# A static order whose estimate puts ScalarE's table loads ahead of the instruction that needs them, with other ranks for the work woven into the projections

## The chip, the cores and the metric

The kernel runs on one core of a Trainium2 chip. The metric is the device time of one execution in microseconds (us). Engines are named as in the profile: PE (TensorE matmul), PEld (TensorE weight load), DVE (VectorE), ACT (ScalarE), POOL (GpSimd) and SP (SyncE, which issues the transfers).

## The reference

One inference step of a decoder trunk with two layers, on a prompt of 1024 tokens and eight samples of four tokens, model width 1024, all in float32.

```python
for layer in range(DEPTH):                       # 2: attention, then gated DeltaNet
    hp, gp = modulate(xp, c_prompt, ...)         # rms_norm(x) * (1 + scale(c)) + shift(c), and gate(c)
    hs, gs = modulate(xs, c_sample, ...)
    if layer % N_MIXERS == 0:
        op, kp, vp = swa_branch(hp, ...)         # q, k, v, z = h @ w_in (16 heads of 64, 4 kv heads)
        osm, ksm, vsm = swa_branch(hs, ..., cache_swa_k, cache_swa_v)
        #   softmax over the last 128 positions with a sink per head; (attn * silu(z)) @ w_out
    else:
        op, cp, sp = gdn_branch(hp, conv0, s0, ...)   # xqkv, z, a, b = h @ w_in; xqkv is 4096 wide
        osm, csm, ssm = gdn_branch(hs, state_gdn_conv, state_gdn_s, ...)
        #   silu(causal conv of 4 taps) gives q, k (8 heads of 128) and v (16 heads of 128);
        #   l2-normed q and k; the delta rule in chunks of 64 with a triangular solve each;
        #   (rms_norm(o) * silu(z)) @ w_out
    xp, xs = xp + gp * op, xs + gs * osm
y_prompt, y_sample = rms_norm(xp, final_norm_g), rms_norm(xs, final_norm_g)
```

The new keys and values, the conv tails and the DeltaNet states are outputs too.

## The kernel before

All 1056 tokens stand on the free axis in three column groups of 384, 384 and 288 (`GRP`). A projection takes 128 output columns at a time: for each group, 24 matmuls add into one bank of PSUM (tile ps_pj). They are 24 because each of the eight blocks of the inner axis is multiplied three times in a split of float32 into a high and a low part: wh with hhi, wh with hlo, wl with hhi (h2hi and h2lo in the second layer). The weights come by transfers into wr and are split into wh and wl by ScalarE and VectorE. A group that is done is evacuated by a function of its own (`evac`), and PE goes on in the next of the two ps_pj banks.

Everything else is woven into this stream of projection matmuls: attention of the heads done so far, the modulation vectors (cT times w_mod, four matmuls a step), the output projection of the attention layer, and in the second layer, for each of eight groups of heads hq, the conv taps, the decays, the chunks' triangular systems (tiles UZ, M, Xd, X), the chain of states (S, uo, ks, DP) and the outputs. Each such piece is a generator, which yields a condition and then issues the next few instructions. `weave` puts it into a list by its rank, and `stages` goes through the list from low ranks to high and runs whatever has its condition fulfilled; the projection calls it (`fetch`, `until`) between its matmuls. Ranks are the numbers in K, in KR for pieces of one head group, and in KT in place of K while the kernel closes.

The conditions come from an estimate that runs along as the program is written. Each instruction that is issued passes `Core.issued`, which is line 84's `call` in the profile for nearly every row. It keeps for every engine the time at which it is free (`self.free`), and for every tile when it was written and last used. `ready(tile)` holds when the estimate has the tile written by the time PE is free; `soon` and `idle` hold a little earlier or later and look at another engine. If the estimate says that a tile is late, PE's matmul on it is written behind more projection matmuls. The order is fixed once the program is built: at run time each engine takes its instructions in that order and waits on semaphores where the estimate was wrong.

ScalarE needs a table load when an Exp follows a Silu or the other way round (`TABLES`).

The pieces that come up below:

- In the second layer a v column goes from ps_pj to XR (a copy on ScalarE), through four taps into vT, then Silu in place (`taps`), and then `turn` transposes it on PE into ps_tr, with the identity in erl, and copies it to vo. There are three vT buffers (VB) and one ps_tr bank; `turn` gives both back.
- In the attention layer the key projection is read twice from its bank: ScalarE casts it to khh, VectorE takes the difference kll.
- Layer 1 is the DeltaNet layer. Its shift and scale come from `modulation_steps`, which multiplies cT by wm, four matmuls a step and eight steps, during the attention; `MM` paces it (a start and a distance, in projection matmuls). Its gate comes from `modulation_gate`, cT times wmod in four steps of four matmuls, during the attention's output projection; `MS` paces it. Behind each step the loads of the next are issued (`load(m + 1)`).
- `SW` is such a pace for the samples' states near the end, and `ORD` the order of q, k, v and z columns in each head group's round.

Of the kernel before, what the change touches and what calls it, by code (L numbers as in the profile page):

```python
# [93 lines left out]
class Core:  # L94
# [15 lines left out]
    def issued(self, eng, op, ins, args, kwargs):  # L110
# [10 lines left out]
        start = self.free[eng]  # L121
        for a in srcs:
            start = max(start, self.after(self.written, a, eng))
            if a.space == PSUM:
                start = max(start, self.after(self.used, a, eng))
        for a in outs:
            if self.used.get(self.key(a), (0.0, ""))[1] != "sync" or eng != "sync":
                start = max(start, self.after(self.used, a, eng))
        if "dma" in op:
            size = 4 * n * outs[0].shape[0] / 1e6  # L130
            rows = max(1, min(2 * outs[0].shape[0], n * outs[0].shape[0] // 16))
            self.free[eng] = start + 0.45
            self.moved = max(start + 0.7, self.moved) + 2.4 * size + 0.0005 * rows
            end = self.moved + self.dl[0 if outs[0].space == DRAM else 1]
        else:
            src = srcs[0] if srcs else outs[0]
            near = src.space == PSUM or srcs[-1].space == PSUM if srcs else False
            rate, fixed, over, seen = 960, 0.155, -0.083, 0.04
            if eng == "tensor":
                m, over, seen, fixed = outs[0].shape[0], 0.0, 0.18, 0.0  # L140
                new, self.group = self.group != outs[0].offset // outs[0].ap[0][0], outs[0].offset // outs[0].ap[0][0]
                if self.kind == "R":
                    rate, fixed = 2326, 0.008 + self.after_f
                    self.after_f = 0.0
                    self.wide_n = 0
                elif self.kind == "T":
                    rate = 1174
                elif m == P:
                    rate, fixed = 592, max(0.0, 0.22 - n / 592)
                elif m == 64:  # L150
                    rate, fixed = (1150 if new else 592), max(0.0, 0.068 - n / 1094)
                elif n >= 256:
                    rate, fixed = (1e9, 0.014) if new and self.wide_n == n else (1200, 0.126)
                elif new:
                    rate, fixed = 1e9, 0.014 if n == self.wide_n else 0.031 if self.wide_n < n else 0.076
                else:
                    rate, fixed = 560, 0.0
                if self.kind != "R":
                    wide = n >= 256 and m >= 64
                    self.after_f = 0.172 if wide else 0.086  # L160
                    self.tail = (-0.181 if wide else -0.08) if m == P else 0.04 if m == 64 else 0.12
                    self.wide_n = n if m < 64 else 0
            elif eng == "scalar":
                rate, fixed, over = 1200, 0.165 if near else 0.195, -0.1
                if any(getattr(kwargs.get(k), "space", None) is not None for k in ("scale", "bias")):
                    fixed += 0.09
                if kwargs.get("accum_out") is not None:
                    over += 0.18
                table = TABLES.get(args[2] if len(args) > 2 else None)
                if table and table != self.table:  # L170
                    self.table, over = table, over + 1.28
            elif eng == "gpsimd":
                rate, fixed, over = 420, 0.07 if n >= 256 else 0.14, 0.0
            elif op == "scalar_tensor_tensor":
                fixed = 0.207 if n > 16 else 0.15
            elif op.startswith("tensor_scalar") and src.space != PSUM:
                rate, fixed = 1920, 0.215 if any(hasattr(x, "tensor") for x in args[2:]) else 0.16
            elif op.startswith("tensor_scalar"):
                fixed = 0.207
            if op == "memset":  # L180
                rate = 1e9
            plain = "tensor_" in op and op not in ("tensor_copy", "tensor_reduce") and all(a.space != PSUM for a in aps)
            if op == "tensor_reduce":
                n *= srcs[0].shape[-1]
            if eng == "gpsimd" and plain:
                start = max(start, self.lock[2])
            elif eng == "vector" and plain and self.lock[0] <= start < self.lock[1]:
                start = self.lock[1]
            end = start + fixed + n / rate
            if eng == "gpsimd" and plain:  # L190
                self.lock[0:2] = start, end
            elif eng == "vector" and plain:
                self.lock[2] = end
            self.free[eng] = end + over
            end += seen
            if eng in self.last:
                self.tc.add_manual_dep(ins, self.last[eng],
                                       mybir.DependencyInfo(mybir.DependencyClass.NoSync, mybir.DependencyReason.DATA),
                                       reason="program order")
            self.last[eng] = ins.name  # L200
# [97 lines left out]
def body(tc, I, O, cst_ap, dbg=None):  # L298
# [21 lines left out]
    AT = (-5, 3)  # L320
    EX = (1.2, 1.6, 0, 0.9)
    ES, EN, EL, EM = EX
    K = {'split': 12, 'add': 26, 'attend': 22, 'turning': 24, 'modulate': 20, 'cached': 8, 'wo': 48, 'turn': 0, 'ahead': 2, 'taps': 2, 'gating': 6, 'decay': 23, 'samples': 28, 'load': 6, 'mod': 6, 'shape': 28, 'decays': 24, 'prepare': 60, 'gather': 23, 'finish': 24, 'states': 40, 'core': 10, 'new': 7}
    KT = {'prepare': 3, 'gather': 25, 'finish': 36, 'states': 10, 'core': 7, 'new': 9, 'load': 18, 'gating': 5, 'samples': 34, 'output': 11}
    KR = [{'chain': 4, 'output': 15, 'solve': 11, 'invert': 19, 'blocks': 31, 'decayed': 22}, {'chain': 31, 'output': 31, 'solve': 13, 'invert': 31, 'blocks': 39, 'decayed': 38}, {'chain': 32, 'output': 2, 'solve': 30, 'invert': 41, 'blocks': 2, 'decayed': 6}, {'chain': 35, 'output': 38, 'solve': 4, 'invert': 4, 'blocks': 0, 'decayed': 23}, {'chain': 9, 'output': 2, 'solve': 23, 'invert': 44, 'blocks': 1, 'decayed': 58}, {'chain': 41, 'output': 36, 'solve': 8, 'invert': 4, 'blocks': 58, 'decayed': 12}, {'chain': 8, 'output': 15, 'solve': 8, 'invert': 12, 'blocks': 58, 'decayed': 12}, {'chain': 10, 'output': 18, 'solve': 42, 'invert': 28, 'blocks': 1, 'decayed': 56}]
    TB = (3, 5)
    SW = (19, 7)
    MS = (54, 12)
    AH, AI = (a / 10 for a in AM)
    GP = (0, 0, 0, 0, 1)  # L330
    ORD = ['zzkv', 'zqzvk', 'zqzkv', 'qzzvk', 'qzzkv', 'vqzzk', 'qzzkv', 'qvzz']
    MM = (11, 4)
    ORDER = [("q", 2), ("q", 3), ("q", 4), ("q", 5), ("z", 0), ("k", 1), ("z", 1), ("z", 2), ("q", 6), ("q", 7),
             ("z", 3), ("z", 4), ("z", 5), ("z", 6), ("z", 7)]
    SE = ("vector", "vector", "vector", "vector")
# [99 lines left out]
    def modulation_gate(l, gw, nw, tag):  # L435
# [29 lines left out]
        def steps():  # L465
            load(0)
            for m in range(KD // 2):
                yield lambda: pos[0] >= MS[0] + MS[1] * (2 * m + 1)
                yield ready(*wts[m])
# [71 lines left out]
    def weave(gen, name, hq=None):  # L541

        rank = KT[name] if nc.closing and name in KT else KR[hq][name] if hq is not None else K[name]
        i = 0
# [466 lines left out]
    if True:  # L1011
# [305 lines left out]
        def cached_rows(b2):  # L1317
# [3 lines left out]
            vc = sa.tile([P, 2, 256], F32, tag="vc", name="vc", bufs=4)  # L1321
            KT = sa.tile([64, 2, 4, P], F32, tag="KT", name="KT", bufs=4)
            nc.sync.dma_start(KT.rearrange("p r h s -> p (r h s)"), I["keysT"][b2])
            nc.sync.dma_start(vc, vc_rows[bs].rearrange("b s c -> s b c"))
            return KT, vc

        def cached_pair(b2, smk, osv, held):

            yield lambda: paired[0] >= b2 - 2
            KT, vc = held[b2] if b2 < 2 else cached_rows(b2)  # L1330
            yield lambda: paired[0] >= b2 - 1
            yield ready(KT)
            lg = yield from bank("lg")
# [125 lines left out]
        load, step, end = modulation_gate(0, at, 8, "wg")  # L1459
# [10 lines left out]
        for t in range(NB + 1):  # L1470
# [3 lines left out]
            for k in range(KD):  # L1474
                hi, lo = wv[k // 2]
                for x, y in ((hhi, hi), (hlo, hi), (hhi, lo)):
                    with pinned():
                        mm = nc.tensor.matmul(pv, x[:, k, t * P:t * P + parts], y[:, k % 2, :],
                                              start=(n == 0), stop=(n == 23))
# [391 lines left out]
    plan = [0]  # L1871
    for r, order in enumerate(ORD):
        pz = [4096 + 2 * r * P, 4096 + (2 * r + 1) * P]
        blocks = {"q": [r * P], "k": [(HQ + r + 1) * P], "v": [2 * HQ * P + 2 * r * P, 2 * HQ * P + (2 * r + 1) * P]}
# [6 lines left out]
    if True:  # L1881
# [498 lines left out]
        states = {0: {}}  # L2380
# [270 lines left out]
        def states_times():  # L2651
# [34 lines left out]
            for u in range(0, len(us_), 2):  # L2686
                b, hd, _ = us_[u]
                if u % 16 == 0:
# [4 lines left out]
                    pk = yield from bank("mi")  # L2693
                yield lambda: pos[0] >= SW[0] + SW[1] * (u + 1) / 10
                yield sure(ES, sts[u], sts[u + 1], zq)
# [368 lines left out]
```

## Time and profile before

| | |
|---|---|
| three runs | 1606.88, 1610.4, 1607.8 us (median 1607.8) |
| profiled execution | 1610.62 us, 2.8 above the median |
| its span, first to last instruction | 1608.8 us; 1.8 us lie outside it |
| mean granted PE clock | 0.996 |
| PE busy | 1581.1 us, 98% |
| DVE, ACT, POOL busy | 76%, 52%, 9% |

A row of the timeline gives the start, the duration, the engine, the instruction with its output and inputs, and in brackets how long the engine had been idle and what ended that. The rows of waits give the engine, its tile, what it waited for, then the sum in us, the number of times and the longest. A busy share alone says little here: PE is the engine that everything is arranged around, so its idle time is what an order can change. fp32 matmuls that are one instruction in the program may show as two in the trace.

### The profile page before, as it was taken

The numbers are of one execution on the slowest core, as the hardware profiler recorded it, in microseconds if no ns is written. First come the engines' busy times: TensorE is split into PE (matmuls) and PEld (weight loads), VectorE is DVE, ScalarE is ACT, GpSimd is POOL, SyncE is SP. The second block draws the span as 40 slices with busy tenths as digits, with TensorE's granted clock in tenths as the row PEclk, the third lists the DMA queues.
The fourth block names the chain that finished last, engine by engine and source line by source line (L and its number), as shares of the span: only waits on it lengthen the run. The fifth ranks groups of instructions, "written<-read, shape, count | busy, mean of one in ns | idle before, by whom it ended". The sixth has DMA issues, their size and how long they took to land. (4 is left out here: it accounts for less than half of the span.)

```text
span 1608.8 us, 30697 instructions
## 1 busy us (share of the span) xinstructions
PE 1581.1 (98%) x10714; PEld 1407.8 (88%) x10714; DVE 1215.7 (76%) x3830; ACT 843.2 (52%) x2422; POOL 145.1 (9%) x231
## 2 busy tenths in 40 slices
PE   9999999999999999999999999999999999999997
PEld 7887888988778999999999999999999998757776
DVE  5726777576676678887988768888688887858787
ACT  4625555454344665466564655755556564524332
POOL 1300000000001002010020100201001002112121
PEclk9999999999999999999999999999999999999999
DMA  9445100106244233242432315314243236685884
GB/s 364 156 148 168 35 29 27 40 26 169 84 141 140 82 99 72 73 117 77 128 69 83 101 53 132 85 52 104 81 115 96 49 83 209 216 265 180 271 284 160
DMA packets 178571, 195.71 MB, mean 122 GB/s; under 512 B 76592, under 2 KB 120464, under 8 KB 178384
## 3 DMA queue, kind: packets, MB, share of 16 engines
q1 hardware_dynamic: 178416, 193.75, 39.9%
q8 instruction: 85, 1.39, 0.4%
q14 instruction: 70, 0.57, 0.1%
HBM read 146.45 MB, written 49.27 MB: 122 GB/s over the span
## 5 line engine op out<-in xcount | busy, mean ns | idle before, releaser
L84 PE MATMUL ps_pj<-h2lo,wh 128*128 128x384 f32 (+1 forms) x1128 | 377.7, 335 | 0.0
L84 PE MATMUL ps_pj<-h2hi,wh 128*128 128x384 f32 (+1 forms) x1128 | 377.7, 335 | 0.0
L84 PE MATMUL ps_pj<-h2hi,wl 128*128 128x384 f32 (+1 forms) x1128 | 375.9, 333 | 0.0
L84 PEld LDWEIGHTS ps_pj<-h2hi,wl 128*128 128x128 f32 x1128 | 213.1, 189 | 2.7 <-DVE wl L84 0.4
L84 PEld LDWEIGHTS ps_pj<-h2hi,wh 128*128 128x128 f32 x1128 | 213.2, 189 | 2.1
L84 PEld LDWEIGHTS ps_pj<-h2lo,wh 128*128 128x128 f32 x1128 | 213.4, 189 | 1.6
L84 PE MATMUL ps_pj<-hhi,wh 128*128 128x384 f32 (+1 forms) x376 | 124.8, 334 | 1.6 <-DVE kll L84 1.0
L84 PE MATMUL ps_pj<-hlo,wh 128*128 128x384 f32 (+1 forms) x376 | 124.6, 334 | 0.1
L84 PE MATMUL ps_pj<-hhi,wl 128*128 128x384 f32 (+1 forms) x376 | 123.6, 332 | 0.0
L84 POOL TENSOR_TENSOR Xd<-Xc,cst 32x128 f32<-32x128 f32 x128 | 67.1, 524 | 459.0 <-DMA Xc<-Xdd 252.7
L84 DVE SCALAR_TENSOR_TENSOR vT<-XR,cT,vT 128x384 f32<-128x384 f32 (+1 forms) x144 | 82.0, 580 | 14.1 <-ACT vT L84 12.9
L84 DVE TENSOR_TENSOR wl<-wr,wh 128x512 fp32r<-128x512 f32 x120 | 83.9, 699 | 10.1 <-ACT wh L84 9.3
L84 ACT CAST wh<-wr 128x512 fp32r<-128x512 f32 x128 | 78.5, 615 | 22.5 <-PE ps_pj L84 21.8
L84 PEld LDWEIGHTS ps_pj<-hlo,wh 128*128 128x128 f32 x376 | 71.4, 190 | 9.7 <-issue 8.8
L84 PEld LDWEIGHTS ps_pj<-hhi,wh 128*128 128x128 f32 x376 | 71.3, 190 | 7.1 <-issue 3.8
L84 PEld LDWEIGHTS ps_pj<-hhi,wl 128*128 128x128 f32 x376 | 71.4, 190 | 4.5 <-issue 4.4
L84 ACT ACTIVATE qe<-ps_mi,Eg 128x128 f32<-128x128 f32 x112 | 35.0, 364 | 67.9 <-PE ps_mi L84 64.8
L84 DVE TENSOR_TENSOR X<-X,tmp 128x126 f32<-128x126 f32 (+22 forms) x248 | 63.8, 257 | 8.5
L84 ACT ACTIVATE prob<-prob,nm 128x256 f32<-128x256 f32 (+1 forms) x128 | 62.3, 490 | 14.8 <-DVE nm L84 14.8
L84 ACT COPY XR<-ps_pj 128x384 f32<-128x384 f32 (+1 forms) x96 | 43.4, 452 | 50.0 <-PE ps_pj L84 49.4
L84 DVE TENSOR_TENSOR tmp<-X 128x126 f32<-128x126 f32 (+22 forms) x248 | 62.4, 252 | 7.3 <-POOL X L84 2.7
L84 POOL TENSOR_TENSOR xt<-xt,y 128x512 f32<-128x512 f32 x30 | 42.9, 1432 | 181.2 <-DVE y L84 176.9
(555 smaller groups left out, 3828.7 us busy)
## 6 DMA issues: line engine op xcount, KB each, us to landing
wr<-in_gwb SPq DMA_DIRECT2D x96, 256.0 KB
S<-in_states SPq DMA_DIRECT2D x42, 256.0 KB
wm<-in_wm SPq DMA_DIRECT2D x16, 512.0 KB
wr<-in_winb SPq DMA_DIRECT2D x32, 256.0 KB
wmod<-in_w_mod SPq DMA_DIRECT2D x32, 256.0 KB
wm<-in_w_mod SPq DMA_DIRECT2D x32, 256.0 KB
DP<-gcr SPq DMA_DIRECT2D x64, 128.0 KB
zl<-zd SPq DMA_DIRECT2D x32, 256.0 KB
```

What stands on the lines that cost most here:

```text
L84: inst = fn(*args, **kwargs)
```

## The change

One line of the estimate moves. Before, an activation that needs another table was entered as done at its usual time, and the engine was held 1.28 us longer behind it. Now its start is put 1.28 us behind the time at which ScalarE is free, so the result of that activation is entered as written 1.28 us later. The instructions themselves do not change; only conditions such as `ready` and `soon` see it. With it come other ranks in K, KT and KR, other paces in SW, MS and MM, and one round in ORD that takes v ahead of the second z.

```diff
                 table = TABLES.get(args[2] if len(args) > 2 else None)
                 if table and table != self.table:
-                    self.table, over = table, over + 1.28
+                    self.table, start = table, max(start, self.free[eng] + 1.28)
...
-    K = {..., 'wo': 48, ..., 'mod': 6, 'shape': 28, 'decays': 24, 'prepare': 60, ..., 'finish': 24, 'states': 40, 'core': 10, 'new': 7}
+    K = {..., 'wo': 60, ..., 'mod': 1, 'shape': 27, 'decays': 35, 'prepare': 61, ..., 'finish': 37, 'states': 7, 'core': 16, 'new': 8}
...
-    SW = (19, 7)
-    MS = (54, 12)
+    SW = (16, 13)
+    MS = (50, 5)
...
-    ORD = ['zzkv', 'zqzvk', 'zqzkv', ...]
-    MM = (11, 4)
+    ORD = ['zzkv', 'zqvzk', 'zqzkv', ...]
+    MM = (11, 12)
```

KT gets other numbers for gather, finish, load, samples and output; KR for one to four of the six pieces in each of the eight head groups.

Both programs issue the same 9020 matmuls on PE and 23 table loads on ACT. They stand in the same order on every engine up to 106 us of the profile before, from 296 to 437, 934 to 1029, 1037 to 1058, 1141 to 1240 and from 1248 us to the end.

The first place is PE near 1240 us, where a group of vT is transposed. Xd times UZ (128x96) belongs to the triangular systems, ps_pj to the projection. Before:

```order
L84 MATMUL ps_lg<-Xd_6458,UZ 128x96 x4
L84 MATMUL ps_pj<-h2lo,wh 128x384
L84 MATMUL ps_pj<-h2hi,wl 128x384
L84 MATMUL ps_pj<-h2hi,wh 128x384
L84 MATMUL ps_tr<-erl,vT 128x128 x3
```

PE at the same place now:

```order
L84 MATMUL ps_lg<-Xd_6460,UZ 128x96 x4
L84 MATMUL ps_pj<-h2lo,wh 128x384
L84 MATMUL ps_pj<-h2hi,wl 128x384
L84 MATMUL ps_pj<-h2hi,wh 128x384
L84 MATMUL ps_pj<-h2lo,wh 128x384
L84 MATMUL ps_pj<-h2hi,wl 128x384
L84 MATMUL ps_pj<-h2hi,wh 128x384
L84 MATMUL ps_pj<-h2lo,wh 128x384
L84 MATMUL ps_pj<-h2hi,wl 128x384
L84 MATMUL ps_pj<-h2hi,wh 128x384
L84 MATMUL ps_pj<-h2lo,wh 128x384
L84 MATMUL ps_tr<-erl,vT 128x128 x3
```

The transposes stand seven projection matmuls later. Counted from the table load ahead of the Silu, 8 matmuls are issued before them here before, and 15 now; at the places near 821, 926 and 1029 us it is 11, 8 and 6 before, and 20, 14 and 13 now.

The second place is PE near 229 us, where the last, 288-wide group of a key projection is followed by the next column's first group of 384. Before, only projection matmuls stand there:

```order
L84 MATMUL ps_pj<-hhi,wh 128x288
L84 MATMUL ps_pj<-hlo,wh 128x288
L84 MATMUL ps_pj<-hhi,wl 128x288
L84 MATMUL ps_pj<-hhi,wh 128x384
L84 MATMUL ps_pj<-hlo,wh 128x384
```

PE there now, with a step of layer 1's modulation (wm, cT) near the group's end:

```order
L84 MATMUL ps_pj<-hhi,wh 128x288
L84 MATMUL ps_tr<-wm,cT 32x512 x4
L84 MATMUL ps_pj<-hlo,wh 128x288
L84 MATMUL ps_pj<-hhi,wl 128x288
L84 MATMUL ps_pj<-hhi,wh 128x384
L84 MATMUL ps_pj<-hlo,wh 128x384
```

PE near that group's beginning now, with the attention's probabilities times values (pT, vsb):

```order
L84 MATMUL ps_pj<-hlo,wh 128x288
L84 MATMUL ps_pj<-hhi,wl 128x288
L84 MATMUL ps_ob<-pT,vsb 64x256 x4
L84 MATMUL ps_pj<-hhi,wh 128x288
L84 MATMUL ps_pj<-hlo,wh 128x288
```

Two fours of other matmuls have moved into the group.

The third place is the queue of transfers on SP, near 445 to 490 us, with the gate's weights (wmod) among rows of x and of the first layer's result (xt, x1d). Before:

```order
L84 DMA x1d<-xt 128x1024
L84 DMA wmod<-in_w_mod 128x512 x4
L84 DMA xt<-in_x_prompt 128x1024 x2
L84 DMA x1d<-xt 128x1024
L84 DMA wmod<-in_w_mod 128x512 x4
L84 DMA cT<-in_taps 128x128
L84 DMA xt<-in_x_prompt 128x1024
L84 DMA x1d<-xt 128x1024
L84 DMA xt<-in_x_prompt 128x1024
L84 DMA wmod<-in_w_mod 128x512 x4
L84 DMA x1d<-xt 128x1024
```

SP there now:

```order
L84 DMA wmod<-in_w_mod 128x512 x4
L84 DMA x1d<-xt 128x1024
L84 DMA xt<-in_x_prompt 128x1024
L84 DMA modG<-in_b_mod 32x512 x2
L84 DMA x1d<-xt 32x1024
L84 DMA x1d<-xt 128x1024
L84 DMA xt<-in_x_prompt 128x1024
L84 DMA wmod<-in_w_mod 128x512 x8
L84 DMA x1d<-xt 128x1024
L84 DMA xt<-in_x_prompt 128x1024
L84 DMA cT<-in_taps 128x128
L84 DMA wmod<-in_w_mod 128x512 x4
```

The loads of two steps stand directly behind one another now, and on PE the four steps lie 38 to 42 matmuls apart instead of 88.

More of the change, by code (lines that the diff above doesn't have):

```diff
@@ L322, in body @@
     ES, EN, EL, EM = EX
-    K = {'split': 12, 'add': 26, 'attend': 22, 'turning': 24, 'modulate': 20, 'cached': 8, 'wo': 48, 'turn': 0, 'ahead': 2, 'taps': 2, 'gating': 6, 'decay': 23, 'samples': 28, 'load': 6, 'mod': 6, 'shape': 28, 'decays': 24, 'prepare': 60, 'gather': 23, 'finish': 24, 'states': 40, 'core': 10, 'new': 7}
-    KT = {'prepare': 3, 'gather': 25, 'finish': 36, 'states': 10, 'core': 7, 'new': 9, 'load': 18, 'gating': 5, 'samples': 34, 'output': 11}
-    KR = [{'chain': 4, 'output': 15, 'solve': 11, 'invert': 19, 'blocks': 31, 'decayed': 22}, {'chain': 31, 'output': 31, 'solve': 13, 'invert': 31, 'blocks': 39, 'decayed': 38}, {'chain': 32, 'output': 2, 'solve': 30, 'invert': 41, 'blocks': 2, 'decayed': 6}, {'chain': 35, 'output': 38, 'solve': 4, 'invert': 4, 'blocks': 0, 'decayed': 23}, {'chain': 9, 'output': 2, 'solve': 23, 'invert': 44, 'blocks': 1, 'decayed': 58}, {'chain': 41, 'output': 36, 'solve': 8, 'invert': 4, 'blocks': 58, 'decayed': 12}, {'chain': 8, 'output': 15, 'solve': 8, 'invert': 12, 'blocks': 58, 'decayed': 12}, {'chain': 10, 'output': 18, 'solve': 42, 'invert': 28, 'blocks': 1, 'decayed': 56}]
+    K = {'split': 12, 'add': 26, 'attend': 22, 'turning': 24, 'modulate': 20, 'cached': 8, 'wo': 60, 'turn': 0, 'ahead': 2, 'taps': 2, 'gating': 6, 'decay': 23, 'samples': 28, 'load': 6, 'mod': 1, 'shape': 27, 'decays': 35, 'prepare': 61, 'gather': 23, 'finish': 37, 'states': 7, 'core': 16, 'new': 8}
@@ new lines, in body @@
+    KT = {'prepare': 3, 'gather': 15, 'finish': 25, 'states': 10, 'core': 7, 'new': 9, 'load': 12, 'gating': 5, 'samples': 30, 'output': 24}
+    KR = [{'chain': 4, 'output': 20, 'solve': 6, 'invert': 19, 'blocks': 31, 'decayed': 22}, {'chain': 31, 'output': 29, 'solve': 13, 'invert': 31, 'blocks': 39, 'decayed': 38}, {'chain': 31, 'output': 2, 'solve': 30, 'invert': 41, 'blocks': 2, 'decayed': 6}, {'chain': 35, 'output': 37, 'solve': 4, 'invert': 4, 'blocks': 10, 'decayed': 23}, {'chain': 14, 'output': 0, 'solve': 23, 'invert': 44, 'blocks': 1, 'decayed': 57}, {'chain': 41, 'output': 36, 'solve': 8, 'invert': 4, 'blocks': 58, 'decayed': 16}, {'chain': 8, 'output': 15, 'solve': 8, 'invert': 12, 'blocks': 57, 'decayed': 12}, {'chain': 10, 'output': 18, 'solve': 42, 'invert': 34, 'blocks': 0, 'decayed': 60}]
@@ L326, in body @@
     TB = (3, 5)
-    SW = (19, 7)
-    MS = (54, 12)
+    SW = (16, 13)
+    MS = (50, 5)
     AH, AI = (a / 10 for a in AM)
     GP = (0, 0, 0, 0, 1)
-    ORD = ['zzkv', 'zqzvk', 'zqzkv', 'qzzvk', 'qzzkv', 'vqzzk', 'qzzkv', 'qvzz']
-    MM = (11, 4)
+    ORD = ['zzkv', 'zqvzk', 'zqzkv', 'qzzvk', 'qzzkv', 'vqzzk', 'qzzkv', 'qvzz']
+    MM = (11, 12)
     ORDER = [("q", 2), ("q", 3), ("q", 4), ("q", 5), ("z", 0), ("k", 1), ("z", 1), ("z", 2), ("q", 6), ("q", 7),
```

## The prediction

> **What bounds the kernel now.** I began with the page's first part, then took the waits of TensorE (PE), then the busy time of the stretches that the change reorders, then the timeline at each wait of PE.
>
> ```profile
> span 1608.8 us, 30697 instructions
> PE 1581.1 (98%) x10714; PEld 1407.8 (88%) x10714; DVE 1215.7 (76%) x3830; ACT 843.2 (52%) x2422; POOL 145.1 (9%) x231
> ```
>
> PE is busy for 98% of the span and executes in the order in which the program issues. An order can gain only what PE idles (1608.8 - 1581.1 = 27.7 us), and lose only by adding idle time. The next view sums PE's waits over the whole span: the engine, its tile and what it waited for, then us in all, times, longest.
>
> ```profile
> PE ps_tr L84 <- ACT vT L84: 2.2, 4, 0.9
> PE ps_lg L84 <- DMA vc<-in_cache_swa_v: 1.1, 1, 1.1
> ...
> PE ps_pj L84 <- DVE kll L84: 1.0, 1, 1.0
> PE ps_mi L84 <- DVE ks L84: 1.0, 1, 1.0
> ```
>
> Not all of it is in reach. Row for row the two programs are the same on every engine up to 106 us of the time before, from 296 to 437, from 934 to 1029, from 1037 to 1058, from 1141 to 1240, and from 1248 to the end. Three windows take in all that is moved, and some of the rest (window, its length, PE busy, and at the end the granted clock, the DMA share and GB/s):
>
> ```profile
> 107.00:286.00 179.00, 177.96 (x1221) 152.46 (x1220) 126.07 (x478) 102.08 (x347) 0.00 (x0) 1.00 0.23 74
> 437.00:935.00 498.00, 495.15 (x3421) 462.05 (x3420) 395.34 (x1235) 280.79 (x782) 42.61 (x87) 1.00 0.35 97
> 1027.00:1246.00 219.00, 216.79 (x1585) 208.07 (x1584) 177.94 (x566) 129.37 (x387) 16.86 (x39) 1.00 0.33 88
> ```
>
> PE idles 179.00 - 177.96 = 1.04, 2.85 and 2.21 us there: 6.1 us, and that is nearly all that this change could win. The vc wait lies at 363.76 us, in an identical stretch, and stays; so does every idle us of the closing part.
>
> **Part 1, the transposes of vT.** A vT column group goes from ScalarE's Silu to a transpose on PE. Four times the Silu is the first after an Exp, so a table load stands ahead of it, which the old estimate did not count. All 23 loads cost the same (busy us, mean ns, idle before):
>
> ```profile
> L84 ACT ACT_TABLE_LOAD x23 | 29.5, 1283 | 4.1 <-DVE AB L84 1.6 <-issue 1.5 <-PEq L3046 0.7
> ```
>
> The timeline at the longest of the four waits (start, us, engine, instruction; in brackets the idle time and who ended it):
>
> ```profile
> 1026.76 0.37 ACT L84 COPY ktok<-ps_lg 128x256 f32<-128x256 f32 x1
> 1027.14 1.28 ACT L84 ACT_TABLE_LOAD   x1
> 1027.28 0.34 PE L84 MATMUL ps_pj<-h2hi,wl 128*128 128x384 f32 x1
> 1027.45 0.34 PE L84 MATMUL ps_pj<-h2hi,wh 128*128 128x384 f32 x1
> 1027.80 0.34 PE L84 MATMUL ps_pj<-h2hi,wl 128*128 128x384 f32 x1
> 1028.44 0.52 ACT L84 ACTIVATE vT<-vT 128x384 f32<-128x384 f32 x1
> 1029.01 0.55 PE L84 MATMUL ps_tr<-erl,vT 128*128 128x128 f32 x3 [0.88 <-ACT vT L84]
> ```
>
> Matmuls of 384 columns start 0.17 us apart (1027.28, 1027.45), so without the wait the transposes would have started at 1027.97: the wait costs 1029.01 - 1027.97 = 1.04 us. The other three, read alike:
>
> ```profile
> 820.71 0.34 PE L84 MATMUL ps_pj<-h2lo,wh 128*128 128x384 f32 x1
> ...
> 821.38 0.44 PE L84 MATMUL ps_tr<-erl,vT 128*128 128x128 f32 x2 [0.33 <-ACT vT L84]
> 925.61 0.33 PE L84 MATMUL ps_pj<-h2hi,wl 128*128 128x384 f32 x1
> ...
> 926.23 0.55 PE L84 MATMUL ps_tr<-erl,vT 128*128 128x128 f32 x3 [0.29 <-ACT vT L84]
> 1238.95 0.33 PE L84 MATMUL ps_pj<-h2hi,wh 128*128 128x384 f32 x1
> ...
> 1239.97 0.55 PE L84 MATMUL ps_tr<-erl,vT 128*128 128x128 f32 x3 [0.69 <-ACT vT L84]
> ```
>
> Less 0.17 each, these are 0.50, 0.45 and 0.85 us. Sum: 1.04 + 0.50 + 0.45 + 0.85 = 2.8 us. From load to transposes the program before issues 11, 8, 6 and 8 matmuls at these four places, the changed one 20, 14, 13 and 15: 9, 6, 7 and 7 more. At 0.17 us a matmul (0.13 for the narrow groups) that covers 0.8 us at the least, against 0.45 at the place with six more, and 1.2 us at the two long ones. All four waits should go: **-2.8 us**. The lower end is the 2.2 us of the wait row above; the upper end is the weight loads' idle time at the same four places, since PE cannot start before its weights:
>
> ```profile
> PEld ps_tr L84 <- ACT vT L84: 3.5, 4, 1.2
> ```
>
> The matmuls that now run ahead of the transposes are work that ran behind them, so they cost nothing of themselves. What is late next is the copy of the transposed column (vo), which DeltaNet's blocks need far behind, and the vT buffer that it frees.
>
> [...]
>
> **Part 2, the bank behind kll.** The key projection's last group is read from its bank in turns by ScalarE (khh) and VectorE (kll), while PE runs only 24 narrow matmuls:
>
> ```profile
> 224.68 0.37 PE L84 MATMUL ps_pj<-hhi,wh 128*128 128x288 f32 x1
> 224.69 0.96 ACT L84 CAST khh<-ps_pj 64x384 fp32r<-64x384 f32 x2 [0.93 <-PE ps_pj L84]
> ...
> 227.80 0.29 PE L84 MATMUL ps_pj<-hhi,wl 128*128 128x288 f32 x1
> 227.83 1.14 DVE L84 TENSOR_TENSOR kll<-ps_pj,khh 64x384 fp32r<-64x384 f32 x2 [1.03 <-ACT khh L84]
> 229.11 0.41 PE L84 MATMUL ps_pj<-hhi,wh 128*128 128x384 f32 x1 [1.02 <-DVE kll L84]
> ```
>
> The group takes 227.80 - 224.68 + 0.13 = 3.2 us and the bank is free at 227.83 + 1.14 = 228.97; PE loses 229.11 - 227.93 = 1.2 us. In the changed order two sets of four matmuls stand inside this group, from the attention and from layer 1's modulation. Each has its price elsewhere in the trace (a four in the program is an x8 here):
>
> ```profile
> 206.55 1.08 PE L84 MATMUL ps_ob<-pT,vsb 128*64 128x256 f32 x8
> ...
> 170.80 1.07 PE L84 MATMUL ps_tr<-wm,cT 128*32 128x512 f32 x8
> ```
>
> About 1.0 us each, 2 us of cover against 1.2 us of wait: **-1.2 us**. The ends are 0 (ScalarE now has a copy of the gate in the same stretch, and khh may start late by as much) and -1.2.
>
> **Part 3, all the rest that moves.** The number of matmuls, their shapes and the changes between plain and split-precision ones are equal but for one, the 23 table loads are still 23, and the transfers are the same ones, some issued earlier: nothing to add. What may change is idle time. Besides vT and kll the three windows hold 6.1 - 2.2 - 1.0 = 2.9 us of it, the 1.0 us behind ks among them, in a place that keeps its order. From below, all of it could go: -2.9. From above, the reordered rows could wait once more for all that the first two windows now lose, 1.04 + 2.85: +3.9. No row says which. Both orders come from the same rules over the same estimate but for one line, so I take what the rows show of such an order now, as much idle time as before: **0**.
>
> Sum: -2.8 - 1.2 + 0 = -4.0 us. The profiled execution took 1610.62 us, 2.8 above the median of 1607.8, so the sum is 1606.6 in its terms and **1603.8 us** in the median's. Ends of the terms: -3.5 - 1.2 - 2.9 = -7.6 (1600.2) and -2.2 + 0 + 3.9 = +1.7 (1609.5).
>
> **The clock.** Two stretches ran at half of it, and how many windows are hit is a matter of the run:
>
> ```profile
> 362.30 0.33 PE L84 MATMUL ps_lg<-kxs,qz 64*32 64x32 f32 x16
> 363.76 0.64 PE L84 MATMUL ps_lg<-KT,qz 64*32 64x128 f32 x16 [1.13 <-DMA vc<-in_cache_swa_v]
> 365.61:372.44 6.83, 6.59 (x48) 6.05 (x35) 3.40 (x14) 2.30 (x9) 0.00 (x0) 0.50 1.02 306
> 536.28:539.69 3.41, 3.41 (x12) 3.41 (x11) 3.16 (x7) 1.70 (x3) 0.00 (x0) 0.50 0.00 0
> ```
>
> At clock 0.50, 3.41 us of PE work are worth 1.7 us. One window more or less moves the time by 1.7 us either way, about the spread of the three runs (1606.88 to 1610.4).
>
> **The rivals.** *The gain is eaten.* Part 3 comes out at its upper end: a transpose that is later holds its vT buffer (there are three) and the one tr bank longer, and other steps that were moved wait in turn. For it: almost 700 us are reordered. Against it: the waits of those stretches are only some seven now, and the new estimate is nearer to the trace's 1.28 us. Time: 1603.8 + 3.9 = 1607.7.
>
> [...]
>
> *Slower: the gate steps outrun their weights.* The four modulation steps of the DeltaNet layer's gate now come every 38 to 42 matmuls instead of every 88. Their loads go out directly behind the step before:
>
> ```profile
> 445.48 1.78 SPq L84 DMA_DIRECT2D wmod<-in_w_mod  x4
> 464.49 1.75 SPq L84 DMA_DIRECT2D wmod<-in_w_mod  x4
> ```
>
> Steps 19.0 us apart become 19.0 x 40 / 88 = 8.6 us apart. One MB at the 306 GB/s of the row of 365.61 is 3.4 us behind 1.8 us of issue, so 3.4 us are left over; the queue must be held up by more than that before PE waits at all. If it is, the nearest row is the vc wait: 1.3 us lost, and the half clock that followed it, half of 6.83 us, 3.4: 4.7 us a time. Two such steps give 1603.8 + 9.4 = 1613.2, one 1608.5. It needs two to be slower.
>
> [...]
>
> **How the numbers follow.** 0.2% is 3.2 us, about what a measurement of this kernel tells from no change: faster is below 1604.6, slower above 1611.0. The forecast (the five waits go, the rest nets out) has 0.55, of which 0.47 lies below 1604.6 and 0.08 above, since a half-clock window or 1 us of new waits is enough. The gain eaten: 0.28 (0.26 within, 0.02 slower). The dear table load: 0.04, within. Late gate steps: 0.13 (two 0.11, slower; one 0.02, within). So faster 0.47, same 0.40, slower 0.13. The range takes the ends of the terms, 1600.2 and 1609.5, the upper with part of a half-clock window: 1600.0 to 1610.5; what it leaves out is the slower rival at its full price and a gain beyond the idle time there is. The forecast's own range is 1600.0 to 1606.0.
>
> **What would show it.** Right: of PE's wait for vT not one of the four is left, and the table loads are still 23 at 1283 ns. Right for part 2: no wait for kll. Part 3 is right if the idle time of the three windows falls from 6.1 to about 2.9 us; wrong if PE has new waits in 437 to 935, each with its releaser's name. The slower rival shows as PE waiting on wmod's transfers near 450 to 490 us, with a clock of 0.50 behind it. If the closing part, with the same rows, changes by over 1 us, the cause is none of these.

## The result, and the profile after

The changed kernel took 1602.0 us (median of 6 runs, 1600.17 to 1603.48) beside 1607.8 us before (6 runs, 1605.14 to 1610.4): a ratio of 0.9964, 95% interval 0.9951 to 0.9976, that is 3.9 to 7.9 us faster. A second measurement, beside 35 runs of the kernel before on another occasion, gave 0.9961 (0.9947 to 0.9976; 1600.4 against 1605.9 us). The forecast was 4.0 us. The profiled execution took 1600.59 us.

The page of the changed kernel, to be read against the two lines quoted of before:

```profile
span 1598.8 us, 30691 instructions
PE 1573.9 (98%) x10714; PEld 1404.9 (88%) x10714; DVE 1215.9 (76%) x3830; ACT 843.0 (53%) x2422; POOL 145.1 (9%) x231
```

The span is 10.0 us shorter, and PE's busy time is 7.2 us shorter with the same number of instructions. Part of that is the clock (0.996 in the mean before, 0.997 now) and part is matmuls that stand closer; both come up below. PE idles 1598.8 - 1573.9 = 24.9 us instead of 27.7. The windows that answer to the three of the prediction (length, then the busy time of PE, PEld, DVE, ACT and POOL with instructions, the granted clock, the DMA share and GB/s):

```profile
106.00:284.40 178.40, 178.40 (x1229) 154.18 (x1228) 126.26 (x475) 104.17 (x349) 0.00 (x0) 1.00 0.23 74
432.00:926.00 494.00, 492.57 (x3416) 461.51 (x3409) 394.61 (x1235) 279.22 (x781) 43.29 (x87) 1.00 0.35 98
1017.00:1237.00 220.00, 219.48 (x1606) 211.40 (x1605) 180.08 (x569) 132.23 (x397) 18.78 (x42) 1.00 0.33 88
```

PE idles 0.00, 1.43 and 0.52 us there, 2.0 us in all, where it was 6.1. (The whole span idles only 2.8 us less: the parts that are the same in both programs idled 1.3 us more in this execution.) The waits of PE over the whole span, its five longest sums and one that was there before:

```profile
PE ps_lg L84 <- ACT sq L84: 1.8, 2, 1.4
PE ps_lg L84 <- DMA vc<-in_cache_swa_v: 1.2, 1, 1.2
PE ps_pj L84 <- DVE y L84: 1.1, 1, 1.1
PE ps_mi L84 <- DVE spare L84: 1.1, 1, 1.1
PE ps_pj L84 <- DVE olo L84: 0.9, 2, 0.5
...
PE ps_tr L84 <- DVE zl L84: 0.6, 2, 0.3
```

There is no row for vT and none for kll any more. What is left at the top lies in the first 110 us, at the samples' keys and in the closing part, where both programs are the same. The place near 1029 us of before now reads (timeline, start, us, engine, instruction):

```profile
1019.53 1.28 ACT L84 ACT_TABLE_LOAD   x1
1020.83 0.53 ACT L84 ACTIVATE vT<-vT 128x384 f32<-128x384 f32 x1
...
1021.40 0.34 PE L84 MATMUL ps_pj<-h2hi,wh 128*128 128x384 f32 x1
1021.58 0.49 PE L84 MATMUL ps_tr<-erl,vT 128*128 128x128 f32 x3
```

The Silu ends at 1021.36 and the transposes start at 1021.58, 0.18 us behind the matmul ahead of them: no wait, and 0.2 us in hand. The bank behind kll, where PE waited until 229.11 us before:

```profile
224.52 1.13 DVE L84 TENSOR_TENSOR kll<-ps_pj,khh 64x384 fp32r<-64x384 f32 x2 [1.03 <-ACT khh L84]
225.42 1.06 PE L84 MATMUL ps_tr<-wm,cT 128*32 128x512 f32 x8
...
226.79 0.34 PE L84 MATMUL ps_pj<-hhi,wh 128*128 128x384 f32 x1
```

The bank is free at 224.52 + 1.13 = 225.65, and PE comes to it at 226.79, 1.1 us later.

### Where the time went, stretch by stretch

The two programs issue the same matmuls on PE, so the start of the same-numbered matmul at the ends of a stretch gives its length in every trace. Where orders differ at such an end, the same number can be another matmul, which moves a length by up to 0.2 us. In us, with the runs that the next section tells of ("vT" is the estimate moved at the four Silus, "MM" the pace MM; "again" is a second profile of the same program):

| stretch (time before) | before | changed | changed again | vT and MM | the same again | vT alone | MM alone | line alone |
|---|---|---|---|---|---|---|---|---|
| 111 to 295 (kll) | 183.9 | 182.4 | 182.4 | 183.7 | 183.7 | 183.9 | 183.7 | 185.0 |
| 362 to 389 (cached keys) | 26.9 | 23.8 | 23.6 | 23.3 | 23.6 | 27.1 | 26.7 | 23.1 |
| 628 to 794 | 165.8 | 164.3 | 164.7 | 166.3 | 164.7 | 166.4 | 166.3 | 165.6 |
| 794 to 932 (two vT waits) | 137.7 | 136.5 | 136.4 | 136.4 | 136.5 | 136.9 | 137.3 | 136.0 |
| 932 to 1137 (one) | 205.0 | 203.9 | 204.1 | 203.4 | 203.4 | 203.7 | 204.3 | 205.5 |
| 1137 to 1242 (one) | 104.6 | 103.5 | 103.5 | 103.7 | 103.6 | 103.6 | 104.6 | 103.8 |

The last three rows hold the vT term: 1.2 + 1.1 + 1.1 = 3.4 us from before to changed. The first holds 1.5 us. Those 4.9 us are in the order. The row of 362 to 389 us is no order (the rows of PE there are the same before and after) but the clock, as the part on it shows. The row of 628 to 794 us differs by 1.6 us between two executions of one and the same program (166.3 and 164.7), so its 1.5 us can't be given to the order.

### The profile page after: what moved, and what is told of

Read it like the earlier page. It is cut to its first block, busy times and chain, and to the rows that moved or that the text cites. A ratio compares the mean times of both kernels' runs of the same rounds, so it can differ in the third digit from the quotient of the medians.

```text
span 1598.8 us, 30691 instructions
## 1 busy us (share of the span) xinstructions
PE 1573.9 (98%) x10714; PEld 1404.9 (88%) x10714; DVE 1215.9 (76%) x3830; ACT 843.0 (53%) x2422; POOL 145.1 (9%) x231
## 5 line engine op out<-in xcount | busy, mean ns | idle before, releaser
L84 DVE TENSOR_TENSOR wl<-wr,wh 128x512 fp32r<-128x512 f32 x120 | 82.9, 691 | 10.6 <-ACT wh L84 9.9
```

The lines of the kernel that those rows point to most:

```text
L84: inst = fn(*args, **kwargs)
```

## The experiments

Ratios are to runs of the kernel before that were made between the others on the same chip; 0.001 is 1.6 us. The mean granted clock of every run is on record too. A run at 0.001 less should take 0.001 x 1606 = 1.6 us more; that is an estimate, and among the 96 runs of before it is 1.4 us.

### The four Silus alone

```diff
-                    self.table, over = table, over + 1.28
+                    self.table, self.loads = table, self.loads + 1
+                    if self.loads in (14, 16, 18, 22):
+                        start = max(start, self.free[eng] + 1.28)
+                    else:
+                        over += 1.28
```

> The kernel before with the table load put ahead in the estimate at the four Silus alone whose transposes waited; ranks and all else as before. Its order is that of the kernel before except for PE's rows near 821 (transposes 7 matmuls later), 926 (2 later), 1029 (7 later) and 1240 us (7 later). Theory (the four waits are the term, -2.8 us): waits for vT gone at 821, 1029 and 1240, about 0.1 to 0.2 us left at 926, nothing else moves: -2.5 us, about 1605.3. Rival (a later transpose holds its vT buffer and the one ps_tr bank, and the wait turns up at what comes next): new waits within some 10 us behind the four places, together 1 us or more, total within 1.5 us of before.

Measured: 1604.6 us, ratio 0.9997 (0.9984 to 1.0010). The trace has no wait of PE for vT left in the whole span. The waits between 815 and 1250 us:

```profile
PE ps_lg L84 <- POOL Xd L84: 0.3, 1, 0.3
PE ps_tr L84 <- ACT XR L84: 0.3, 1, 0.3
PE ps_tr L84 <- DVE zl L84: 0.2, 1, 0.2
PE ps_lg L84 <- DVE mo L84: 0.2, 1, 0.2
```

XR's and mo's 0.5 us were not there before; Xd's is as it was, and zl's is down from 0.6 us. So 0.5 us at most moved on to later steps, and the stretches of the table give 0.8 + 1.3 + 1.0 = 3.1 us. The time did not show them: the interval reaches from 2.6 us faster to 1.6 us slower. Part of what hides them is the clock: its mean over these 12 runs was 0.9965, and 0.9973 over the 32 of before, which is 1.3 us. With that taken out the mean is 1.9 us below before, from 0.7 to 3.0.

### MM alone

```diff
-    MM = (11, 4)
+    MM = (11, 12)
```

> The kernel before with MM = (11, 12) alone. Its order differs from before only between 116 and 290 us; the group behind kll has the two fours of other matmuls in it, as in the changed kernel. Theory (cover): the 1.2 us wait for kll is gone and nothing comes in its place: -1.2 us, about 1606.6. Rival (khh starts late because ScalarE has other work there, the wait stays): -0.3 to 0.

Measured: 1604.9 us, ratio 0.9993 (0.9979 to 1.0007). PE's waits from 107 to 290 us:

```profile
PE ps_mi L84 <- DVE prob L84: 0.6, 1, 0.6
```

The wait for kll is gone, as the two fours cover it, and a new one stands at 151 us: the transposes of the attention's probabilities wait for VectorE's last scaling of prob. By start times it costs 0.76 + 0.19 us there, and the whole stretch is only 0.2 us shorter. Neither theory had that: the cover works, and the gain is given back 77 us earlier. In the order before, a step of the modulation is PE's 865th to 868th matmul, ahead of those transposes; with MM alone the nearest steps are the 837th and the 989th. That this 1.0 us of work was prob's cover fits both orders, but it was not tried by itself and is not shown.

### Both, and the changed kernel beside them

The two edits above together:

> Both of the above and nothing else: -2.5 - 1.2 = -3.7 us if the terms add, about 1604.1. What the changed kernel has beyond it (5.8 - 3.7 = 2.1 us by the medians) is then the third term, the other ranks. Rival (the two terms are the whole change and the rest nets to nothing): as fast as the changed kernel, 1602.

Measured: 1600.0 us, ratio 0.9967 (0.9956 to 0.9979). That was as the rival had it, and so it was run again beside the changed kernel:

> The changed kernel once more, beside the next run on the same chip, to split the third term from chance. Theory (by the stretches of the two profiles the other ranks bring a term of their own, about -2.4 us): about 1600.0 where before is 1605.8, 1 to 3 us faster than the run of the two terms alone. Rival (the two terms are all of it): equal to that run within 1 us.

> The four Silus and MM alone, once more on the same chip as the changed kernel. Theory: -3.7 us or less against before (in the run with MM alone 1.0 us came back as a wait for prob), so 1602 to 1603 where the changed kernel takes 1600. Rival: as fast as the changed kernel.

Measured: the changed kernel 1600.4 us, ratio 0.9961 (0.9947 to 0.9976); the two edits 1601.4 us, ratio 0.9969 (0.9954 to 0.9983). The intervals lie on each other; if the ranks bring anything beyond the two edits, it is about 1 us. The traces place it: 183.7 against 182.4 us from 111 to 295 us, which is prob's wait (0.6 us in the trace of the two edits, none in the changed kernel), and no gain in the DeltaNet part, where the other ranks are 0.7 us slower if anything (136.5 against 136.4, 203.4 against 204.1). With the clock taken out as above, the means of the two edits are 4.0 and 3.9 us below before, and that of the changed kernel 4.6 (4.1 in the first measurement, against all 96 runs of before). The theory of a third term of 2.4 us fell: over all the reordered rows, what the other ranks are seen to bring is that they keep the first 1.3 us from being lost.

### The four Silus back

The changed kernel, with the old estimate at those four loads and the new one at the other 19.

> The changed kernel with the old estimate at the four Silus alone; its ranks stay. Its order is that of the changed kernel up to 820 us and in most of the rest; the transposes stand earlier by 9, 19 (another order there), 7 and 7 matmuls. Theory: the waits for vT come back at two to four places, 0.4 to 1.0 us each: +2.3 to +2.8 against the changed kernel, about 1604.6. Rival (the other ranks alone would have moved them): within 0.8 us of the changed kernel.

Measured: 1609.7 us, ratio 1.0025 (1.0013 to 1.0038), 4 us slower than before, where the changed kernel is 5.5 to 5.8 us faster. PE's waits from 810 to 1245 us:

```profile
PE ps_tr L84 <- ACT vT L84: 5.5, 4, 3.8
PE ps_tr L84 <- DVE zl L84: 0.6, 2, 0.3
```

All four are back, and one is 3.8 us long. PE stands still from 911.13 us, while ScalarE still has most of four exponentials of DP (the first from 910.84), the load and the Silu to do:

```profile
911.38 1.65 ACT L84 ACTIVATE DP<-DP 128x512 f32<-128x512 f32 x3
913.05 1.28 ACT L84 ACT_TABLE_LOAD   x1
914.34 0.52 ACT L84 ACTIVATE vT<-vT 128x384 f32<-128x384 f32 x1
914.92 0.90 PE L84 MATMUL ps_tr<-erl,vT 128*128 128x128 f32 x3 [3.79 <-ACT vT L84]
```

In this profile the clock falls to half at 913.67 us, during that wait, for 6.83 us, and this is no single case: 11 of the 12 runs had a mean granted clock of 0.996 or less, against 23 of the 96 of before. The mean over the 12 was 0.9952, and 0.9973 over the 32 of before beside them, which is 3.4 us. With that taken out the mean is 0.9 us above before, so about 5 us above the changed kernel, which is the size of the waits. The mechanism was right and the size was not: the wait is a load plus whatever stands ahead of it on ScalarE, and here the clock came on top.

### The line alone, the ranks alone

The kernel before with the new line in all 23 places and its old ranks:

> The kernel before with the one line of the estimate alone, old ranks. The transposes of vT then stand later after every load, by 20, 7, 8 and 15 matmuls from the four loads' places as far as the order can be matched, and one four of other matmuls lies in the group behind kll. Theory (the line brings the vT term, the ranks the third): no wait for vT (-2.8), 0.2 us left of kll's 1.2 (-1.0), and new waits of 1 to 2 us in the stretches that nobody has arranged again: -2 to -3 us against before. Rival (the line is all of the change): as fast as the changed kernel, -5.8.

The changed kernel with the old line:

> The changed kernel with the old line in all 23 places: ranks and paces alone. Theory: kll's wait stays away (-1.2 against before), waits for vT are back at two to four places; after the run with four Silus of the old kind, one of them may be long (3.8 us there, where three exponentials of DP and a load stood ahead of the Silu): between -2 and +4 us against before, slower than the changed kernel by 2 us or more. Rival (the ranks are all of the change): within 1 us of the changed kernel.

Measured: the line alone 1605.3 us, ratio 1.0001 (0.9988 to 1.0014); the ranks alone 1617.6 us, ratio 1.0068 (1.0050 to 1.0087). PE's waits with the line alone, from 107 to 1246 us:

```profile
PE ps_pj L84 <- DVE wl L84: 2.0, 1, 2.0
PE ps_mi L84 <- ACT uo L84: 1.6, 1, 1.6
PE ps_pj L84 <- DVE kll L84: 1.3, 1, 1.3
PE ps_mi L84 <- ACT kx L84: 0.7, 1, 0.7
```

vT's four waits are gone. The four longest that stand there now come to 5.6 us; kll's is among them, because the four of the attention stands just ahead of that group and not in it, and those for wl, uo and kx are new. The time is that of before, and the 2 to 3 us that the theory expected did not come. This is the rival "the gain is eaten", in the kernel where the ranks were left. The ranks alone, from 620 to 1130 us:

```profile
PE ps_lg L84 <- ACT jk L84: 2.3, 1, 2.3
PE ps_tr L84 <- ACT vT L84: 2.1, 3, 1.1
PE ps_lg L84 <- DVE UZ L84: 2.1, 4, 0.9
PE ps_pj L84 <- DVE wl L84: 1.6, 1, 1.6
```

Ranks that were set under one estimate and are played under the other cost 11.6 us against before, where the theory had 4 at the most. Neither half of the change is a gain by itself that these runs show.

### The paces back

The changed kernel with MS = (54, 12):

> The changed kernel with MS = (54, 12) again: the gate's steps 88 matmuls apart instead of 38 to 42. PE's order is that of the changed kernel up to 431 and from 923 us, new between. Theory (the close steps cost nothing, since PE does not wait for wmod in the changed kernel, but the DeltaNet stretch behind gets an order that its ranks were not set for): slower than the changed kernel by 0.5 to 4 us, all of it between 620 and 923 us. Rival (the close steps or their loads cost something that shows elsewhere): faster than the changed kernel.

Measured: 1611.1 us, ratio 1.0029 (1.0016 to 1.0041), 10.6 us slower than the changed kernel. By start times 11.3 us lie between 542 and 922 us, behind the gate's steps and not at them; 1.7 us of that is the clock, which is at half for 3.41 us from 843.65 us in this profile. PE's waits from 541 to 923 us, the longest four:

```profile
PE ps_tr L84 <- ACT vT L84: 1.5, 1, 1.5
PE ps_ob L84 <- DVE UZ L84: 1.4, 1, 1.4
PE ps_lg L84 <- DVE tmp L84: 1.3, 1, 1.3
PE ps_mi L84 <- DVE vo L84: 1.2, 1, 1.2
```

The theory's place was right and its size far too small. In the changed kernel PE waits for nothing between 425 and 500 us, so four steps 9 us apart did not outrun their loads.

The changed kernel with MM = (11, 4):

> The changed kernel with MM = (11, 4) again. Order differs only from 116 to 290 us; in the group behind kll stands one four of other matmuls (ps_ob) and no longer two. Theory (cover): 1.0 us of the 1.2 is covered by the one four, 0.2 to 0.3 us of wait left for kll; +0.2 to +0.4 us against the changed kernel in that stretch. Rival (the steps of the modulation are the cover): 0.8 us or more of wait for kll is back.

Measured: 1604.6 us, ratio 0.9991 (0.9979 to 1.0004). PE's waits from 107 to 290 us:

```profile
PE ps_pj L84 <- DVE kll L84: 1.3, 1, 1.3
PE ps_mi L84 <- ACT kx L84: 0.7, 1, 0.7
PE ps_lg L84 <- DVE mx L84: 0.2, 1, 0.2
```

kll's wait is back in full. I had read the order wrongly in that expectation: the four of the attention (ps_ob) stands ahead of the 24 matmuls there, not among them. With nothing in the group there is no cover, and the stretch is 2.5 us longer. So the two fours inside the group are what takes the wait away.

### The clock behind the cached keys

In both kernels PE waits for the samples' cached keys and values near 362 us, with small matmuls (64x32, 64x128) before and after. One condition was moved, in the changed kernel and in the one before:

```diff
-            yield ready(KT)
+            yield sure(2.5, KT)
```

> The changed kernel with one condition moved: the samples' attention takes its cached keys 2.5 us later by the estimate (sure(2.5, KT) in place of ready(KT)). Order differs only in PE's rows from 359 to 395 us. Theory (the wait of 1.3 us there, with small matmuls around it, brings a window of half clock in a share of the executions): wait gone, -1.3 us, and no half clock near 365 us in any execution, so -1.3 to -3 us and a narrower spread. Rival (half clock comes by itself): -1.3 us or less and the same spread.

> The kernel before with the same single condition moved. The profile of before had 6.83 us at half clock behind this wait, worth 3.4 us. Theory: -1.3 us for the wait and up to 3.4 us for the clock in the executions that had it: median -2 to -4.5 us, spread well below before's 8.5 us (1602.2 to 1610.7). Rival: -1.3 us, spread unchanged.

Measured: 1601.7 us, ratio 0.9975 (0.9965 to 0.9985), in the changed kernel (0.9961 and 0.9964 without the edit); 1605.5 us, ratio 0.9992 (0.9981 to 1.0004), in the one before. Neither is a gain that can be told from none. The wait for KT went, and one for sp, the same attention's next step, came (0.9 and 1.7 us). No half clock was seen at this place in either profile. Before's runs from 1602.6 to 1608.6 us were closer together than those without the edit (1602.6 to 1612.4), and the mean granted clock was 0.9975 with the edit, in both kernels, and 0.9972 in the runs of before beside them. That is weak evidence, from 12 runs each against 29, and 0.5 us at most.

What the traces show is when the clock falls there. With vT alone, the timeline and then the window (with the granted clock behind PE, PEld, DVE, ACT and POOL):

```profile
363.81 0.33 PE L84 MATMUL ps_lg<-kxs,qz 64*32 64x32 f32 x16
365.56 0.64 PE L84 MATMUL ps_lg<-KT,qz 64*32 64x128 f32 x16 [1.42 <-DMA vc<-in_cache_swa_v]
...
366.54:373.38 6.84, 6.84 (x51) 5.97 (x50) 2.83 (x14) 1.75 (x6) 0.00 (x0) 0.50 1.08 323
```

The changed kernel at the same rows:

```profile
360.44 0.33 PE L84 MATMUL ps_lg<-kxs,qz 64*32 64x32 f32 x16
361.93 0.64 PE L84 MATMUL ps_lg<-KT,qz 64*32 64x128 f32 x16 [1.16 <-DMA vc<-in_cache_swa_v]
...
361.12:367.95 6.83, 5.98 (x72) 5.26 (x73) 1.05 (x5) 0.99 (x4) 0.00 (x0) 1.00 1.07 266
```

All of the clock's steps lie multiples of 3.41 us apart within one execution (365.61, 372.44, 536.28 and 539.69 us of before: 2, 48 and 1 of them), and where that grid lies differs from one to the next (a step at 365.61 us of before, at 366.54 with vT alone). Five of the fourteen profiles have the clock at half here: before, vT alone, MM alone, Silus back and MM back. In all five the 3.41 us window that ends with the fall began between 0.7 us before and 0.3 us after the first small matmul, and PE idled for 1.13 to 1.53 us ahead of KT's matmuls. In each of the nine others at least one of the two was missing. In the two profiles of the changed kernel PE idled for 1.16 and 1.00 us, but a window began 0.7 and 0.4 us after that matmul, and the clock stayed up. In the second profile of the two edits a window began 0.25 us before it, but PE idled for 0.62 us only, and the clock stayed up too. The length of this stretch in the table, 26.7 to 27.1 us or 23.1 to 23.8, is mostly that fall: 3.3 us, by the place of the grid and the lateness of a transfer.

Nothing shows that the changed order makes it rarer. The mean granted clock was 0.9972 over the 18 runs of the changed kernel and 0.9971 over the 96 of before.

## Why the prediction was right, step by step

**The bound.** PE's idle time was what could be won, and the three windows fell from 6.1 to 2.0 us of it, where the text said about 2.9. (The second profile of the changed kernel has 2.1.) The stretches gave more than that idle time, 4.9 against 4.1 us, so idle time is not quite all that an order can win; part 1 has a reason. The identical part behind 1248 us contributed nothing here: from 1242 us to PE's last matmul it takes 358.0 us in both profiles. The second profile of the changed kernel has 356.9 for the same rows, so the 1 us that the prediction set as a sign is within what executions differ by.

**Part 1, the transposes.** Foreseen -2.8; measured 3.4 us in the three stretches, and 3.1 with the four Silus alone. All four waits went, the loads stayed 23 at 1283 ns, and little took the waits' place. The term was a little too small. One reason shows: behind a wait the three transposes took 0.31 us to the next matmul (1029.01 to 1029.32), and without one 0.24 (1021.58 to 1021.82), which the reading of the wait alone leaves out; four times 0.07 is 0.3 us. The Silu started 0.02 us behind the load again (1019.53 + 1.28, 1020.83), and the transposes at 1021.58 did not wait. That a matmul does not start before its weights, on which the upper end rested, is what both traces have: taken in order, each of the 10714 matmuls starts 1 to 428 ns after the start of its weight load.

**Part 2, kll.** Foreseen -1.2; the stretch gives -1.5, and the cover is confirmed from both sides (MM alone, MM back). What the working missed is that the steps of the modulation are taken away from somewhere else: with the pace alone prob's wait came up, and the stretch gained 0.2 us and not 1.2. The number held because prob does not wait in the changed kernel, with its other ranks. Nothing in the working foresaw that, so in this term the size is in part luck.

**Part 3, the rest.** Foreseen 0 between -2.9 and +3.9; by the order about 0 (the changed kernel against the two edits: 1 us by the medians, 1.3 us won at prob, up to 0.7 us lost in the DeltaNet part). It was taken as 0 because no row said more. The runs show that this 0 does not come by itself: with MM, MS, the line at the four Silus or the whole line put back into the changed kernel, the stretches of the table other than the cached keys' come out 2.6 to 16 us longer, part of it at half clock. So the reason that the prediction gave (the same rules give as much idle time as before) is not borne out. As far as the runs show, the number came right because the new ranks go with the new line. The reordered parts are also 786 us by the prediction's own bounds, and not almost 700.

**The sum.** -4.0 foreseen, 4.9 by the stretches, 5.5 to 5.8 by the medians. In the second measurement the rest is about what the clock gives: its mean was 0.9972 over the 12 runs of the changed kernel and 0.9967 over the 35 of before, and 0.0005 of 1606 us is 0.8 us. Over all the runs the two kernels' clocks are the same, so that part is chance and no gain of the order.

**The rivals.** "The gain is eaten" is what the line alone does. Of the dear table load, which has 0.04 of the chances, no run shows a cost beyond the load's row: in the profiles of before and after, ScalarE's next instruction starts 0.01 to 0.02 us behind 21 of the 23 loads, all four at vT among them, and behind the other two it waits for a transfer (zo<-in_xT) and for VectorE (qT). Late gate steps did not come: PE has no wait there. Of the half clock, the text had the price (1.7 us a window, in either direction) and that it was a matter of the run; the profiled execution of before had 3.4 us of it behind the cached keys and that of after none, which is most of why the two profiles lie 10.0 us apart where the medians lie 5.8 apart. Another 1.5 us is the row of 628 to 794 us.

## What to carry to other kernels

In a statically ordered program, look for waits that recur behind the same rare event (a table load, the third buffer, the turn of a bank): an estimate that books its cost on the wrong side can show as the same short wait at several of them (four of the 23 loads here), and moving a few matmuls ahead of the consumer took it away at no cost that the stretches show. Work that is moved to hide a wait leaves a place behind, and a wait can come up there: look at both ends. And a table of ranks belongs to the estimate under which it was set: the new line with the old ranks gained nothing, and the new ranks with the old line cost 11.6 us. Moving the estimate only where the waits were, with one pace beside it, kept the old ranks and had most of the gain.

## What the runs showed of the hardware that was not expected

The granted clock fell to half in the middle of the kernel, at 365.61 and 536.28 us of before, and PE's longest wait in that whole profile is 1.13 us. All five falls near the cached keys came with 1.1 to 1.5 us of waiting among matmuls of 64x32 and 64x128, in a 3.41 us window that began between 0.7 us before and 0.3 us after the first of them, and the fall cost 3.3 us. Near 536 us of before it fell with no wait at all, at 536.28, at the end of a window in which PE had this row:

```profile
533.18 2.14 PE L84 MATMUL ps_lg<-erl,abT 64*128 64x32 f32 x18
```

Matmuls with outputs of 64x32 stand ahead of the fall at both places; that they bring it is not shown.

The same program at the same rows differs from one execution to another by 1.6 us in 166 (628 to 794 us, the two edits): PE waits 1.6 us for ks in one and not at all in the other. Ahead of it VectorE waited 1.74 against 0.17 us for X, which GpSimd writes only behind a transfer (X<-Ld; 4.55 against 2.90 us of waiting there). A single profile can't settle a difference of that size.
